# First stage of an attention and convolution backbone: c's rows on another queue, earlier weight roundings, context tiles on ScalarE, ropes on VectorE, and gates ahead of queries

## The chip, the core and the metric

The kernel runs on one core of a Trainium2 chip. The metric is the device time in microseconds of one execution on that core, from its start to its end. Engines are named as in the profile: PE (TensorE, the matmuls), DVE (VectorE), ACT (ScalarE), POOL (GpSimd) and SP (SyncE, which here only issues transfers). DMA transfers are issued by an engine into its own queue; this kernel uses SP's and ACT's.

## The reference

Two layers work on 1024 latent tokens `x` and 256 context tokens `ctx`, both 1024 wide. Layer 0 is attention with 16 query heads in 4 groups that share keys and values (head width 128); layer 1 is a convolution module. What matters here is the way into layer 0:

```python
# per layer: x += gate * Mixer(RMSNorm(x) * (1 + scale) + shift)
# (shift, scale, gate) = Linear_i(SiLU(c))      for latent tokens
# (shift, scale, gate) = Linear_i(SiLU(c_ctx))  for context tokens
proj = h_lat @ w_in
q = apply_rope(split_heads(proj[..., :q_end], N_Q_HEADS), cos, sin)
k = apply_rope(split_heads(proj[..., q_end:k_end], N_KV_HEADS), cos, sin)
v = split_heads(proj[..., k_end:v_end], N_KV_HEADS)
z = proj[..., v_end:]
kv_c = h_ctx @ w_in[:, q_end:v_end]
o = windowed_attention(q, k, v, kc, vc, sink)
y = (o * jax.nn.silu(z)) @ w_out

def apply_rope(x, cos, sin):       # x1, x2: the halves of a head
    return concatenate([x1 * cs - x2 * sn, x2 * cs + x1 * sn])
```

All of it is fp32. `z` is the gate of a head's output.

## The kernel before, in words

**Precision.** PE's fast fp32 format (F32R) keeps fewer bits, so a value is split into a rounded high part and the low part that is left (`whi`/`wlo` for weights, `hh`/`hl` for x, `hch`/`hcl` for the context, `kh`/`kl` and `qh`/`ql` for keys and queries, `ahi`/`alo` for the modulation weights). The high part is a copy on ACT, the low part a subtraction (`split_lo`) on DVE or POOL. A product is three matmuls (`mm3`): high by high, high by low, low by high.

**Memory.** SBUF is handed out in 45 pages of 1024 words and 6 halves of 528 (`Pages`); a tile's name carries `page` or `half` and, in the listings of the order, its running number. PSUM tiles are `pss` (two of two banks), `psg` (two) and `pso` (two).

**Order.** Between `pin("PVAG")` (L334) and `pin("P")` (L607) PE, DVE, ACT and POOL keep the order in which the code is written: this is the first stage. Behind it only PE keeps the written order, and a scheduler places the instructions of the others. Every instruction is recorded at line 90, where a helper issues it, so groups are told apart by their tiles.

**The first stage.** SP loads half of x's rows (`xs0`), the weights of modulation block 0 (`ada_load`, `araw`), weight chunks, and so on in the order in which it is written. ACT's queue loads `c`, `c_ctx`, the identity, the norm weights, `sel` and `sink` (L174 to L179). The rows of `c`, `c_ctx` and the norm weights lie in one tile, `crow`. PE runs five fillers (`idle`: matmuls of zeros `zr` by zeros, 128 x 512, whose result nobody reads), turns `crow` into columns (one transpose), and ACT makes SiLU of it. 28 more fillers follow (L342). Then:

- `ada_mm(pr)` multiplies the columns with four pages of modulation weights, for one of four blocks `pr` of 256 channels. A few of these pages are used as plain fp32 (`ADA_FP`: all of block 0 and two each of blocks 1 and 2), the others are split by `ada_split`. The result is a row of 512 in PSUM, copied to the tile `arow` half by DVE and half by ACT. `ada_cols` turns it into columns `mod` (shift and scale).
- `square` and `normalise` scale rows of x or ctx by 1/rms, `turn` transposes them by PE, and `x_tiles` scales and shifts the result by `mod` on DVE (`hf`), rounds on ACT (`hh`) and subtracts on DVE (`hl`). `c_tile` does the same for a context tile, whose low part is made on POOL (tiles 0 to 5) or DVE (tiles 6 and 7).
- `x_mm(kt, half, acc, which)` adds K tile `kt` (of 8) to the projections k, q and v of the first group, for one half of the tokens (512).
- `WStream` streams weight chunks of 128 columns. `wsA.load()` issues a load on SP, `wsA.split()` rounds the next chunk on ACT and subtracts on DVE (chunks 1 to 3) or POOL; with a list as argument it leaves the subtraction to a later call. The first three chunks are k, q and v of group 0.
- `rope_start` copies a projection out of PSUM by ACT, issues two transfers on ACT's queue that swap the halves of the head (the rotated copy, `rope_half<-rope_half` or `rope_page<-rope_page`, 64 x 512 each), and multiplies by the cosine on DVE. `rope_end` multiplies the rotated copy by the sine on POOL, adds on DVE, rounds on ACT and subtracts on POOL.

The code of the stage ends with the ropes of the first half (k and q, L601), the last x projections, and the split of the fourth weight chunk.

**Behind the stage.** From L1107 on, `enqueue` lists the chunks of the next projections, in the order in which they were added to the list of chunks (L269 to L280), and `fill(n)` runs n matmuls of that list. Nine such matmuls of the fourth chunk run first (`fill(9)`, L1111); behind them come the context's products with k and v of group 0 (`gemm_ctx`, 24 matmuls of 256 columns each), the ends of the first ropes, and the turn of v (`tails`, whose source is `vf`). Then come 16 heads of 8 query blocks each: `scores` two blocks ahead, fillers of 12 projection matmuls in each step of the first four heads, softmax, `pv`. Before, a head's list is q of the next head and then the gate z of this one; two steps before head h + 1 begins, what is left of its q is run (`fill(1000, ...)`). From head 1 on, `low_parts` (L717) also sends the low parts of layer 0's output weights and of the convolution's to DRAM.

## Time and profile before

| | |
|---|---|
| time, 3 runs | median 1775.41 us (1773.73 to 1775.61) |
| the profiled execution | 1776.85 us, of which the span of the profile is 1775.0 |
| mean clock granted to PE | 0.994 |
| PE busy | 1729.6 us, 97% of the span |
| DVE, POOL, ACT busy | 1143.9, 922.2 and 861.6 us |
| PE's share of the first of 40 slices (44.4 us) | 8 tenths |
| HBM traffic | 188.70 MB read, 41.69 MB written, 130 GB/s over the span |

The profile is one execution, taken apart by a hardware profiler; the times of the runs come without it. Its views are a page of totals, and answers of the trace: the waits of an engine (what it waited for, by tile), the timeline of an engine in a window, tables of short windows with the granted clock of PE, and a tile's own instructions. A row of a timeline has the start, the duration, the engine, the operation with the tile written and the tiles read, the number of like instructions in the row, and in brackets how long the engine was idle before it and what ended that. ACTq and SPq are the instructions by which ACT and SP issue transfers.

### The profile page before, as it was taken

What the parts mean: (1) busy time and instruction counts of PE and PEld (TensorE: products, weight loads), DVE (VectorE), ACT (ScalarE), POOL (GpSimd) and SP (SyncE); (2) the same over time, 40 slices, a digit from 0 to 9 for tenths busy, and PEclk for the clock granted to TensorE, in tenths of its full rate; (3) what the DMA queues carried; (4) which work ended last, traced back from release to release, by engine and by line L of the source; (5) the groups of instructions that cost most, each with busy time, mean ns of one, the idle gap of its engine ahead of it and who ended that gap; (6) DMA issues with size and microseconds to landing.
All of it is one profiled execution on the core that took longest, in us unless ns stands there. A gap on an engine that the chain in (4) does not pass through costs nothing.

```text
span 1775.0 us, 23838 instructions
## 1 busy us (share of the span) xinstructions
PE 1729.6 (97%) x8420; PEld 1425.6 (80%) x8420; DVE 1143.9 (64%) x2076; ACT 861.6 (49%) x1409; POOL 922.2 (52%) x836
## 2 busy tenths in 40 slices
PE   8989899999999999999999999999999999999997
PEld 4668788888888888887888888888888888787886
DVE  3755553665556554565314269999999999867833
ACT  5444353545444443444433445564656565466741
POOL 0155555666556646662100247998988888121400
PEclk9989999999999999999999999999999999999999
DMA  9233443354434542435777733011121212377871
GB/s 318 83 94 107 126 136 89 113 166 138 122 107 131 161 145 66 135 105 185 266 260 244 261 95 107 25 48 36 36 84 36 84 36 72 124 244 238 310 281 48
DMA packets 195324, 242.45 MB, mean 137 GB/s; under 512 B 11798, under 2 KB 126790, under 8 KB 195204
## 3 DMA queue, kind: packets, MB, share of 16 engines
q1 hardware_dynamic: 188164, 230.01, 39.7%
q10 hardware_dynamic: 7040, 10.91, 2.5%
q8 instruction: 66, 1.08, 0.3%
q14 instruction: 54, 0.44, 0.1%
HBM read 188.70 MB, written 41.69 MB: 130 GB/s over the span
## 4 chain that ended last, share of the span: by engine, by line
PE 69%; DMA 3%; DVE 2%; issue 1%; ACT 1%; POOL 1%; ACTq 0%; SPq 0%; DVEq 0%; POOLq 0%
PE psg L90 34%; PE pss L90 17%; PE pso L90 17%; DMA low_page<-in_conv_w_out_dram 1%; DMA rope_half<-rope_half 1%; DMA ozf_page<-ozd 1%; DVE mask_page L90 1%; DMA wo_page<-in_conv_w_out_dram 0%; POOL rope_half L90 0%; DVE p_page L90 0%; DVE rope_half L90 0%; DVE ptlo L90 0%; DMA wolC<-low_page 0%; DMA dww_raw<-in_ada_w_dram 0%; POOL p_page L90 0%
## 5 line engine op out<-in xcount | busy, mean ns | idle before, releaser
L90 POOL TENSOR_TENSOR odd_half<-odd_half,prod_half 128x513 f32<-128x513 f32 (+2 forms) x252 | 313.0, 1250 | 24.2 <-ACT prod_half L90 10.9
L90 PE MATMUL psg<-hh_page,whi_page 128*128 128x512 f32 x608 | 241.3, 397 | 3.1 <-ACT whi_page L90 3.1
L90 PE MATMUL psg<-hh_page,wlo_page 128*128 128x512 f32 x608 | 240.5, 396 | 3.5 <-DVE wlo_page L90 3.5
L90 POOL TENSOR_TENSOR wlo_page<-wraw_page,whi_page 128x1024 fp32r<-128x1024 f32 x71 | 175.5, 2473 | 125.8 <-ACT whi_page L90 88.6
L90 PE MATMUL psg<-hl_page,whi_page 128*128 128x512 f32 x608 | 240.4, 395 | 0.0
L90 ACT ACTIVATE prod_half<-ubuf,dww 128x513 f32<-128x513 f32 (+2 forms) x252 | 165.3, 674 | 110.5 <-POOL odd_half L90 108.3
L90 PE MATMUL psg<-h2h_page,whi_page 128*128 128x512 f32 x464 | 184.0, 396 | 0.0
L90 PE MATMUL psg<-h2l_page,whi_page 128*128 128x512 f32 x464 | 182.8, 394 | 0.0
L90 PE MATMUL psg<-h2h_page,wlo_page 128*128 128x512 f32 x464 | 182.5, 393 | 0.0
L90 POOL TENSOR_SCALAR p_page<-p_page,sc 128x640 f32<-128x640 f32 (+1 forms) x128 | 100.9, 789 | 145.9 <-DVE sc L90 145.2
L90 DVE SCALAR_TENSOR_TENSOR pss<-ubuf,dww,pss 128x512 f32<-128x512 f32 (+3 forms) x270 | 172.6, 672 | 0.1
L90 DVE SCALAR_TENSOR_TENSOR pss<-ubuf,wsum,pss 128x512 f32<-128x512 f32 (+3 forms) x270 | 171.9, 672 | 0.2
L90 ACT ACTIVATE p_page<-p_page,sc 128x641 f32<-128x641 f32 (+1 forms) x128 | 102.7, 802 | 92.9 <-DVE sc L90 73.7
L90 ACT ACTIVATE pthi<-pss 128x640 fp32r<-128x640 f32 (+1 forms) x144 | 88.7, 616 | 114.9 <-PE pss L90 106.0
L90 DVE TENSOR_TENSOR ptlo<-pss,pthi 128x640 fp32r<-128x640 f32 (+1 forms) x144 | 103.2, 716 | 63.5 <-ACT pthi L90 62.5
L90 PEld LDWEIGHTS psg<-hh_page,wlo_page 128*128 128x128 f32 x608 | 114.9, 189 | 27.7 <-DVE wlo_page L90 4.3
L90 PEld LDWEIGHTS psg<-hh_page,whi_page 128*128 128x128 f32 x608 | 114.8, 189 | 26.2 <-ACT whi_page L90 3.5
L90 PEld LDWEIGHTS psg<-hl_page,whi_page 128*128 128x128 f32 x608 | 115.1, 189 | 21.5
L90 ACT ACTIVATE whi_page<-wraw_page 128x1024 fp32r<-128x1024 f32 x88 | 92.5, 1052 | 63.9 <-PE psg L90 29.1
L90 PE MATMUL pso<-h2h_page,whi_page 128*128 128x512 f32 x304 | 119.7, 394 | 0.0
L90 PE MATMUL pso<-h2l_page,whi_page 128*128 128x512 f32 x304 | 119.6, 393 | 0.0
L90 PE MATMUL pso<-h2h_page,wlo_page 128*128 128x512 f32 x304 | 119.5, 393 | 0.0
(256 smaller groups left out, 4079.0 us busy)
## 6 DMA issues: line engine op xcount, KB each, us to landing
wraw_page<-in_conv_w_in_dram SPq DMA_DIRECT2D x48, 512.0 KB, 4.0
wraw_page<-in_attn_w_in_dram SPq DMA_DIRECT2D x40, 512.0 KB, 4.6
wol_page<-wolA SPq DMA_DIRECT2D x32, 512.0 KB, 5.5
wo_page<-in_attn_w_out_dram SPq DMA_DIRECT2D x32, 512.0 KB, 7.4
wo_page<-in_conv_w_out_dram SPq DMA_DIRECT2D x32, 512.0 KB, 5.7
wol_page<-wolC SPq DMA_DIRECT2D x32, 512.0 KB, 6.8
rope_half<-rope_half ACTq DMA_DIRECT2D x76, 128.0 KB, 2.5
araw_page<-in_ada_w_dram SPq DMA_DIRECT2D x32, 256.0 KB, 5.8
```

What stands on the lines that cost most here:

```text
L90: r = f(*a, **k)
```

## The change

All of it concerns the order of work and the engine that does it; the arithmetic stays.

1. The loads of `c` and `c_ctx` move from ACT's queue to SP's, ahead of x's rows.
2. `idle(28)` becomes `idle(29)`, and `idle(4)` behind `ada_split(1)` goes.
3. The first two weight splits move ahead of `ada_mm(0)`, and the copy of a modulation row is made by DVE alone, 512 wide.
4. The two split pages of modulation block 2 are made together (earlier for the second), the first two of block 3 behind the x tiles of K tile 4 instead of ahead of `ada_cols(2)`.
5. Context tiles are scaled and shifted on ACT (Identity with scale and bias) instead of DVE.
6. The fourth weight chunk is split right behind the last `x_tiles` instead of ahead of `x_mm(7, 1)`.
7. The first four ropes have their product with the sine and their last subtraction on DVE instead of POOL.
8. In the first group (heads 0 to 3) a head's gate z is projected ahead of the next head's q: the chunk list and the places that enqueue agree on it.

```diff
-    A.dma_start(out=crow[0:8], in_=c.rearrange("o (r p) -> (o r) p", p=P))
-    A.dma_start(out=crow[8:16], in_=c_ctx.rearrange("(r p) -> r p", p=P))
+    SY.dma_start(out=crow[0:8], in_=c.rearrange("o (r p) -> (o r) p", p=P))
+    SY.dma_start(out=crow[8:16], in_=c_ctx.rearrange("(r p) -> r p", p=P))
...
-            zq.insert(1 if h % 4 == 3 else 0, (("q", h + 1), wcol((h + 1) * P)))
+            zq.insert(1 if h < 4 or h % 4 == 3 else 0, (("q", h + 1), wcol((h + 1) * P)))
...
-    idle(28)
+    idle(29)
...
-            V.tensor_copy(R[pr][0:4, 0:256], o[0:4, 0:256])
-            act(R[pr][0:4, 256:512], o[0:4, 256:512], AF.Copy)
+            V.tensor_copy(R[pr][0:4, 0:512], o[0:4])
...
-        modulated(turn(cx, kt, lambda: ps_o(bank))[:, 0:CT], [(h, l, lambda f: f[:, 0:CT])],
-                  m[:, 2 + i, 1:2], m[:, i, 1:2], CT, V if kt >= 6 else G)
+        tp = turn(cx, kt, lambda: ps_o(bank))
+        f = pg.alloc(F32, [1024], "hf")
+        act(f[:, 0:CT], tp[:, 0:CT], AF.Identity, scale=m[:, 2 + i, 1:2], bias=m[:, i, 1:2])
+        act(h, f[:, 0:CT], AF.Copy)
+        split_lo(V if kt >= 6 else G, l, f[:, 0:CT], h)
+        pg.free(f)
...
-    def rope_end(started, sl, dh, dl, eng):
+    def rope_end(started, sl, dh, dl, eng, rest=G):
         pool, pgs, w, r = started
-        tt(G, w, w, sin[:, sl], ALU.mult)
+        tt(rest, w, w, sin[:, sl], ALU.mult)
         tt(eng, r, r, w, ALU.add)
         act(dh, r, AF.Copy)
-        split_lo(G, dl, r, dh)
+        split_lo(rest, dl, r, dh)
...
+    low = []
+    wsA.split()
+    wsA.split(low)
     ada_mm(0)
     tps = [turn(xs0, kt, lambda: acc1[kt]) for kt in range(2)]
-    wsA.split()
     ada_cols(0)
-    low = []
-    wsA.split(low)
     x_tiles((tps[0], 0, 0, V), (tps[1], 1, 0, V))
     low.pop()()
     ada_split(1)
-    idle(4)
...
-    ada_split(2, (2,))
+    ada_split(2)
...
-    ada_split(2, (3,))
...
-    ada_split(3, range(2))
...
     x_tiles((tp, 4, 0, V), (tq, 4, 1, V))
+    ada_split(3, range(2))
...
     x_tiles((tp, 6, 1, V), (tq, 7, 1, V))
+    wsA.split()
     pg.free(*xs1)
...
-    wsA.split()
     x_mm(7, 1, acc1, range(3))
     pin("P")
...
+    enqueue(("z", 0))
     enqueue(("q", 1))
-    enqueue(("z", 0))
     fill(9)
...
-    rope_end(rk0, lo, *(t[:, lo] for t in d0[0]), V)
+    rope_end(rk0, lo, *(t[:, lo] for t in d0[0]), V, V)
...
-                for key in ((("z", n), ("q", n + 1)) if n % 4 == 3 else (("q", n + 1), ("z", n))):
+                for key in ((("z", n), ("q", n + 1)) if n < 4 or n % 4 == 3 else (("q", n + 1), ("z", n))):
```

Three places show how instructions move. The first is the beginning of the program on ACT, then on SP; `crow` holds the rows of c, c_ctx and the norm weights. ACT before:

```order
L90 DMA crow_half_75<-in_c_dram 8x128
L90 DMA crow_half_75<-in_c_ctx_dram 8x128
L90 DMA ident<-in_k_ident_dram 128x128
L90 DMA crow_half_75<-in_norm_g_dram 16x128
L90 DMA sel<-in_k_sel_dram 128x2
L90 DMA sink<-in_attn_sink_dram 128x16
```

SP now:

```order
L90 DMA crow_half_75<-in_c_dram 8x128
L90 DMA crow_half_75<-in_c_ctx_dram 8x128
L90 DMA x_page_84<-in_x_dram 128x1024
L90 DMA x_page_85<-in_x_dram 128x1024
L90 DMA x_page_86<-in_x_dram 128x1024
L90 DMA x_page_87<-in_x_dram 128x1024
```

The two rows of c stand at the head of SP's queue, ahead of x's four; on ACT's, the identity is now first and the norm weights second.

The second place is ACT at the end of the stage: `hch` are the context's high parts, `vf` a copy of v, `rope` the copies for the ropes, and `whi<-wraw` the rounding of the fourth weight chunk. Before:

```order
L90 ACTIVATE hch_page_756<-hf_page_761 128x256
L90 ACTIVATE hch_page_756<-hf_page_768 128x256
L90 ACTIVATE rope_half_772<-pss_157 128x512
L90 DMA rope_half_773<-rope_half_772 64x512 x2
L90 ACTIVATE rope_page_779<-pss_157 128x512
L90 DMA rope_page_780<-rope_page_779 64x512 x2
L90 ACTIVATE hch_page_756<-hf_page_798 128x256
L90 ACTIVATE vf_half_888<-psg_161 128x512
L90 ACTIVATE hch_page_756<-hf_page_805 128x256
L90 ACTIVATE whi_page_809<-wraw_page_714 128x1024
```

Now:

```order
L90 ACTIVATE hh_page_679<-hf_page_718 128x512
L90 ACTIVATE hh_page_684<-hf_page_721 128x512
L90 ACTIVATE whi_page_726<-wraw_page_707 128x1024
L90 ACTIVATE hf_page_733<-pso_730,mod_206 128x256
L90 ACTIVATE hch_page_642<-hf_page_733 128x256
L90 ACTIVATE hf_page_740<-pso_737,mod_206 128x256
L90 ACTIVATE vf_half_836<-psg_160 128x512
L90 ACTIVATE hch_page_642<-hf_page_740 128x256
```

The rounding of the chunk stands right behind the last two roundings of x (`hh`), ahead of the last four context tiles and of the rope copies; each context tile now has two rows on ACT, `hf` and `hch`.

The third place is DVE at the same time: `rope` with `cos` and `sin` are the products, `rope<-rope,rope` the sums, `hcl` the low parts of context tiles 6 and 7, and `wlo` that of the fourth chunk. Before:

```order
L90 TENSOR_TENSOR rope_half_774<-pss_157,cos_page_580 128x512
L90 TENSOR_TENSOR rope_page_781<-pss_157,cos_page_580 128x512
L90 TENSOR_SCALAR hf_page_798<-pso_795,mod_207 128x256
L90 TENSOR_TENSOR hcl_page_757<-hf_page_798,hch_page_756 128x256
L90 TENSOR_SCALAR hf_page_805<-pso_802,mod_207 128x256
L90 TENSOR_TENSOR rope_half_774<-rope_half_774,rope_half_773 128x512
L90 TENSOR_TENSOR hcl_page_757<-hf_page_805,hch_page_756 128x256
L90 TENSOR_TENSOR rope_page_781<-rope_page_781,rope_page_780 128x512
L90 TENSOR_TENSOR wlo_page_810<-wraw_page_714,whi_page_809 128x1024
```

Now:

```order
L90 TENSOR_TENSOR wlo_page_727<-wraw_page_707,whi_page_726 128x1024
L90 TENSOR_TENSOR rope_half_771<-pss_157,cos_page_574 128x512
L90 TENSOR_TENSOR rope_page_778<-pss_157,cos_page_574 128x512
L90 TENSOR_TENSOR rope_half_770<-rope_half_770,sin_page_575 128x512
L90 TENSOR_TENSOR rope_half_771<-rope_half_771,rope_half_770 128x512
L90 TENSOR_TENSOR rope_page_777<-rope_page_777,sin_page_575 128x512
L90 TENSOR_TENSOR hcl_page_754<-hf_page_795,hch_page_753 128x256
L90 TENSOR_TENSOR rope_page_888<-pss_158,cos_page_574 128x512
L90 TENSOR_TENSOR rope_page_778<-rope_page_778,rope_page_777 128x512
L90 TENSOR_TENSOR kl_page_830<-rope_half_771,kh_page_829 128x512
L90 TENSOR_TENSOR hcl_page_754<-hf_page_802,hch_page_753 128x256
```

The chunk's low part stands ahead of all ropes; the low parts of context tiles 6 and 7 stand behind products with the sine, and the second behind a rope's last subtraction (`kl`), which were POOL's before.

More of the change, by code (lines that the diff above doesn't have):

```diff
@@ L1113, in backbone_kernel @@
     run(gemm_ctx(wsA.hl[0], o))
-    rope_end(rk0, lo, *(t[:, lo] for t in d0[0]), V)
+    rope_end(rk0, lo, *(t[:, lo] for t in d0[0]), V, V)
     tails.append(finish("v", 0, 1, acc1[2], d0[2]))
-    rope_end(rq0, lo, *(t[:, lo] for t in d0[1]), V)
+    rope_end(rq0, lo, *(t[:, lo] for t in d0[1]), V, V)
     rq1 = rope_start(acc1[1], hi, pg)
@@ L1122, in backbone_kernel @@
     tails.append(finish("v", 0, 2, o, d0[2]))
-    rope_end(rq1, hi, *(t[:, hi] for t in d0[1]), V)
-    rope_end(rk1, hi, *(t[:, hi] for t in d0[0]), V)
+    rope_end(rq1, hi, *(t[:, hi] for t in d0[1]), V, V)
+    rope_end(rk1, hi, *(t[:, hi] for t in d0[0]), V, V)
     for i in range(3):
```

## The prediction

> **What bounds the kernel now.** I read the page first, then PE's waits up to 130 us, then the timelines of that stretch by engine, and last PE's waits later on.
>
> ```profile
> PE 1729.6 (97%) x8420; PEld 1425.6 (80%) x8420; DVE 1143.9 (64%) x2076; ACT 861.6 (49%) x1409; POOL 922.2 (52%) x836
> ```
>
> PE is busy for 97% of the span, so only time in which PE waits, runs slowly, or runs fillers can be won. The list of PE's waits up to 130 us (us in total, times, longest) shows where the first stage loses it:
>
> ```profile
> PE psg L90 <- DVE wlo_page L90: 3.5, 1, 3.5
> PE psg L90 <- DMA crow_half<-in_norm_g_dram: 3.3, 1, 3.3
> PE psg L90 <- ACT whi_page L90: 3.1, 1, 3.1
> PE pso L90 <- ACT vf_half L90: 2.2, 1, 2.2
> ...
> PE pso L90 <- DVE mod L90: 1.4, 1, 1.4
> ```
>
> Two places matter. The first is the start, in PE's timeline (start, us, engine, operation):
>
> ```profile
> 1.92 2.50 PE L90 MATMUL psg<-zr_half 128*128 128x512 f32 x5 [1.92 <-DVE zr_half L90]
> 7.75 0.28 PE L90 MATMUL psg<-ident,crow_half 32*128 32x32 f32 x1 [3.33 <-DMA crow_half<-in_norm_g_dram]
> 7.97 8.27 PE L90 MATMUL psg<-zr_half 128*128 128x512 f32 x28
> 16.17 7.03 PE L90 MATMUL pso<-araw_page,cf 128*4 128x512 f32 x16
> 23.13 1.10 PE L90 MATMUL pss<-ident,x_page 128*128 128x128 f32 x8
> ```
>
> PE turns c's rows at 7.75, after their last transfer, then runs 28 fillers, and only behind those the first modulation matmuls (16.17 to 23.13). Everything later in the stage hangs on 23.13. The second place is the end of the stage, again PE's timeline:
>
> ```profile
> 90.36 0.39 PE L90 MATMUL psg<-hl_page,whi_page 128*128 128x512 f32 x1
> 90.59 0.40 PE L90 MATMUL psg<-hh_page,wlo_page 128*128 128x512 f32 x1
> ...
> 105.06 0.28 PE L90 MATMUL pso<-hch_page,wlo_page 128*128 128x256 f32 x1
> 105.18 0.28 PE L90 MATMUL pso<-hch_page,whi_page 128*128 128x256 f32 x1
> ...
> 112.12 0.66 PE L90 MATMUL pso<-ident,vf_half 128*128 128x128 f32 x4 [2.18 <-ACT vf_half L90]
> ```
>
> Between 90.98 (the end of the x projections) and 112.12 PE has 15 matmuls of 512 columns and 48 of 256. Starts lie 0.23 and 0.12 apart when nothing is awaited, so this is 15 x 0.23 + 48 x 0.12 = 9.2 us of work in 21.1 us: 11.9 us are lost. 8.8 of them are the waits for whi, wlo and vf above. The rest is a slow clock behind those waits, by the table of windows (next to last: granted clock):
>
> ```profile
> 100.00:102.00 2.00, 2.00 (x7) 1.52 (x6) 0.80 (x2) 0.60 (x1) 0.00 (x0) 0.50 0.55 119
> ```
>
> The timeline of all engines shows why the fourth weight chunk came so late:
>
> ```profile
> 92.95 1.04 ACT L90 ACTIVATE whi_page<-wraw_page 128x1024 fp32r<-128x1024 f32 x1
> 93.30 0.69 DVE L90 TENSOR_TENSOR rope_half<-rope_half,rope_half 128x512 f32<-128x512 f32 x1 [0.70 <-POOL rope_half L90]
> ...
> 94.59 1.27 POOL L90 TENSOR_TENSOR rope_page<-rope_page,sin_page 128x512 f32<-128x512 f32 x1 [1.32 <-DMA rope_page<-rope_page]
> ...
> 95.81 1.26 POOL L90 TENSOR_TENSOR kl_page<-rope_half,kh_page 128x512 fp32r<-128x512 f32 x1
> 95.89 1.73 DVE L90 TENSOR_TENSOR rope_page<-rope_page,rope_page 128x512 f32<-128x512 f32 x1 [1.56 <-POOL rope_page L90]
> 97.54 1.21 DVE L90 TENSOR_TENSOR wlo_page<-wraw_page,whi_page 128x1024 fp32r<-128x1024 f32 x1
> ```
>
> The chunk's rounding (whi) stands on ACT behind the copies and transfers of the first ropes, and its low half (wlo) on DVE behind a rope's sum, which waits for POOL's product with the sine.
>
> **The change part by part.** Times below are on before's clock.
>
> *c's rows from SP.* ACT's own start and the landing of a rotated copy (64 x 512 floats; view of the rope tile, 85 to 116 us):
>
> ```profile
> 1.37 0.28 ACTq L90 DMA_DIRECT2D crow_half<-in_c_ctx_dram  x1
> 1.68 0.36 ACTq L90 DMA_DIRECT2D ident<-in_k_ident_dram  x1
> 2.08 0.45 ACTq L90 DMA_DIRECT2D crow_half<-in_norm_g_dram  x1
> ```
>
> ```profile
> DMA to landing us min/median/max: 2.9/3.5/4.1
> ```
>
> The norm weights, which end the wait, were issued at 2.08, behind three of the four large row transfers, and were there at 7.7: 5.6 us. Now they are ACT's second transfer, so at about 1.37, and the rows of x start behind c's two on SP. At 2.9 us they land at 4.3, and PE turns c when its first five fillers end, at 4.42. At 5.6 us they land at 7.0. I take the first, since the large transfers no longer run ahead of them. The 29 fillers then begin at 4.65. As slow at their start as the 28 were (8.20), with one more of 0.23, they end at 13.1; all at 0.23 they end at 11.3. The modulation matmuls take 6.96 more: 18.3 to 20.1. Their data bound this: SP issued the transfers of these weights up to 10.72 (the last six in its timeline, 0.54 each), and they land after (view of their tile)
>
> ```profile
> 7.92 3.26 SPq L90 DMA_DIRECT2D araw_page<-in_ada_w_dram  x6
> ...
> DMA to landing us min/median/max: 4.3/5.8/7.1
> ```
>
> that is by 17.8, or 18.7 behind two small issues (0.9 us). The last quarter of the matmuls (1.74) would then end at 20.4 at the latest. I take 19.4: a gain of 3.7 us against 23.13, with 2.7 to 4.8 as bounds, and 0.5 if the norm weights still need 5.6 us (7.04 + 0.22 + 8.43 + 6.96 = 22.65).
>
> The Trainium skill has a rule on the fillers ("TensorE: Matmul & The Clock Gate", Part 1): PE's clock is halved after an idle window of about 3.4 us and full again after as long a busy one. By it the 3.3 us gap at 4.42 cost a second slow start; without the gap the fillers could end at about 11.6, and the sum would be 1 us better than mine. The row of 28 fillers (8.27 us instead of 28 x 0.23 = 6.4) agrees.
>
> *Weight roundings ahead, one copy of the modulation row on DVE, four fillers fewer.* In the first three rows these stand in ACT's idle time before 23.13. The path from there (turns, columns, scale, rounding) is the same. I cost them at 0, between 0.2 lost (one 512-wide copy for two halves) and 0.3 won.
>
> *Middle of the stage.* The waits for mod (1.4) and two smaller ones go, since two roundings of the last modulation block now stand behind the x tiles of block 4. But DVE does as much as before, and the same roundings must be done for PE's last modulation block:
>
> ```profile
> 69.58 2.36 DVE L90 TENSOR_TENSOR alo_page<-araw_page,ahi_page 128x1024 fp32r<-128x1024 f32 x2 [0.26 <-ACT ahi_page L90]
> ```
>
> ```profile
> 74.25 1.52 POOL L90 TENSOR_SCALAR x_page<-x_page,r 128x1024 f32<-128x1024 f32 x1 [46.76 <-DVE r L90]
> ```
>
> Replayed in the new order with DVE's own durations, these two end at 72.0, as before (71.9), and the context rows are scaled at 75.9 (before 75.8), which PE then awaits. So I take 0; the bound is 2.2 won, if DVE were not the limit.
>
> *Context tiles on ACT, fourth chunk early, ropes on DVE.* The chunk's whi now follows the last x rounding on ACT (84 to 85) and its low half ends near 86, well before 91: the waits of 3.1 and 3.5 and the slow clock go, and with them the whole 11.9, unless something else is late. It is: context tiles 6 and 7 have their low halves on DVE behind the ropes. PE would reach their matmuls at 95.4 and 96.6. ACT issues q's rotated copy up to 92.9 (second transfer at 92.25; lands 2.9 later, 95.15); DVE's product (0.69) and then tile 6's half end at 96.2: 0.8 us of wait. Tile 7's half stands behind three more operations of 0.69 and ends at 98.5: 1.9 us. PE is through both context products at 101.7, and turns v at 103.05 instead of 112.12 (bank freed at 102.2): 9.1 us won. Bounds: 11.9 with no wait, 6.0 if the copies land after 4.1 us (1.2 for each of two) and the clock falls behind these waits (3.4 us at half speed, the rest of the bound).
>
> In the rows above DVE's sum took 1.73 us beside POOL's subtraction and 0.69 alone. The Trainium skill ("SBUF — State Buffer", Who interferes with whom) says that a DVE operation with two SBUF inputs blocks against a POOL operation that reads SBUF; the two rows agree. By this rule the eight rope operations stay at 0.69, as I count them, since the change leaves POOL no rope work there; at 1.73 each the sum would be some 4 us worse.
>
> *Gate leads.* In the first four heads the matmuls are as many, but head h+1's q now comes behind gate h. Its first half ends near step 3 of 8 and is wanted at step 6.
>
> ```profile
> 146.57 0.36 PE L90 MATMUL pss<-kh_page,qh_page 128*128 128x256 f32 x1
> ```
>
> ```profile
> 214.44 0.57 ACT L90 ACTIVATE rope_half<-psg 128x512 f32<-128x512 f32 x1
> ```
>
> ```profile
> 226.46 1.31 POOL L90 TENSOR_TENSOR ql_page<-rope_half,qh_page 128x512 fp32r<-128x512 f32 x1
> ```
>
> By before's steps the half would end at 133.7 and be wanted at 146.6: 12.9 us, against up to 13.3 for a rope (214.44 to 227.77). So 0 to 0.4 for each of three heads. The stall here that the reshuffled rows may remove is
>
> ```profile
> 212.71 1.23 PE L90 MATMUL pss<-ident,p_page 128*128 128x128 f32 x5 [3.35 <-DVE sc L90]
> ```
>
> which I leave at 0 both ways, with 4.5 won (3.4 and its slow clock) as a bound.
>
> **Sum.** 3.7 + 0 + 9.1 + 0 = 12.8 us. The profiled execution took 1776.85 us (span 1775.0 and 1.85 around it); the median of the runs is 1775.41. 1776.85 - 12.8 = 1764.05, and from the median **1762.6**.
>
> **The rivals.** (1) The norm weights still land late: 0.5 + 9.1 = 9.6, 1765.8. For it: the queues share engines that were full at that time. Against: the big transfers start later. (2) Context halves wait longer on the rope copies: 3.7 + 6.0 = 9.7 at the bound, and 1768 if a wait of the middle comes back as well (1.4 and 1.0 in ACT's longer queue). (3) The stall at 212 goes too: 12.8 + 4.5, 1758.1. (4) The other side: gate leads starves the scores. Place: the first scores of heads 1, 2 and 3, for want of q. Price: whatever a rope takes over 12.9 us, three times, with 1.7 us of slow clock behind each. From 15.5 us a rope (2.6 + 1.7, three times) it eats the gain; at 19 us it costs 3 x (6.1 + 1.7) = 23.4 and gives 1786.0. For it: POOL works off these ropes between the softmax's rows. Against: the slowest rope seen took 13.3.
>
> **How the numbers follow.** A measurement of this kernel can tell about 0.2%, 3.6 us, from no change. Chances: forecast 0.58, (1) 0.15, (2) 0.12, (3) 0.09, (4) 0.06. Cases that win over 3.6 us hold 0.94; of these I move 0.01 to "same" for the stretch between (2) and (4), and of (4) 0.01. So faster 0.93, same 0.02, slower 0.05. The forecast's own range is 1759.5 to 1765, from its bounds. Taking in (1), most of (2) and (3) gives 1757.5 to 1768.5, which leaves out (4) and the edges.
>
> **What would show it.** Right: PE turns c before 5 us; the x rows are turned near 19.4 instead of 23.13, and the first x matmul comes as much earlier; the last modulation matmuls still wait about 2 us on alo; no wait on whi or wlo of the fourth chunk, the clock full from 90 us on, and small waits on hcl instead; v turned near 99 on the new clock. Wrong: c turned after 7 us; waits over 4 us for hcl or rope tiles; scores of heads 1 to 3 waiting on ql.

## The result and the profile after

| | before | after |
|---|---|---|
| time | 1775.51 us median of 4 runs (1773.73 to 1778.43) | 1756.86 us median of 4 runs (1756.38 to 1762.61) |
| ratio of the times | | 0.9901, 95% interval 0.9876 to 0.9925 |
| the profiled execution, its span | 1776.85, 1775.0 us | 1756.40, 1754.2 us |
| mean clock granted to PE | 0.994 | 0.995 |

The change wins 18.65 us between the medians; the ratio makes 17.6 of it, with 13.3 to 22.0 as its interval. 12.8 were forecast, just below that interval. By the ratio the time stands at 1757.8 on the scale of the prediction, at the lower edge of its range (1757.5 to 1768.5); the median itself lies 0.6 below it. The changed kernel was measured a second time, beside other kernels: 1757.76 us, ratio 0.9891 (0.9879 to 0.9904).

The waits of PE up to 130 us in the changed kernel (columns: us in total, times, longest):

```profile
PE pso L90 <- DVE vl_page L90: 2.1, 1, 2.1
...
PE pss L90 <- ACT hh_page L90: 1.9, 1, 1.9
PE pso L90 <- DVE hcl_page L90: 1.5, 1, 1.5
PE pso L90 <- ACT hh_page L90: 0.7, 1, 0.7
PE pso L90 <- POOL x_page L90: 0.7, 1, 0.7
PE pso L90 <- DVE alo_page L90: 0.6, 1, 0.6
```

The waits for the norm weights, for whi and wlo of the fourth chunk, for mod and for the copy of v are gone. New are one for `vl` (the low part of v, 2.1), a longer one for the first rounded x (`hh`, 1.9, before 0.8), one for `hcl`, and two of 0.7 in the middle of the stage (a second `hh`, and rows scaled by POOL). PE's timeline at the start:

```profile
1.92 2.50 PE L90 MATMUL psg<-zr_half 128*128 128x512 f32 x5 [1.92 <-DVE zr_half L90]
4.34 0.31 PE L90 MATMUL psg<-ident,crow_half 32*128 32x32 f32 x1
4.59 8.30 PE L90 MATMUL psg<-zr_half 128*128 128x512 f32 x29
12.82 7.03 PE L90 MATMUL pso<-araw_page,cf 128*4 128x512 f32 x16
19.78 1.09 PE L90 MATMUL pss<-ident,x_page 128*128 128x128 f32 x8
20.80 1.05 PE L90 MATMUL pso<-sel,arow_half 5*128 5x2 f32 x8
23.74 0.50 PE L90 MATMUL pss<-hh_page,whi_page 128*128 128x512 f32 x1 [1.89 <-ACT hh_page L90]
```

c is turned at 4.34 without a wait, x at 19.78. Behind the columns (20.80) PE now waits 1.89 us where before it ran the four fillers and then waited 0.77. The table of short windows of the changed kernel (the last three columns are the granted clock, the DMA share and GB/s) shows what follows, and the same again near 77 us:

```profile
24.00:26.00 2.00, 1.78 (x5) 1.26 (x5) 1.97 (x3) 1.27 (x2) 0.00 (x0) 0.69 1.11 341
26.00:28.00 2.00, 2.00 (x4) 0.25 (x4) 1.71 (x3) 1.26 (x2) 0.00 (x0) 0.50 1.19 326
...
76.00:78.00 2.00, 2.00 (x11) 1.80 (x9) 0.57 (x1) 0.65 (x2) 0.96 (x2) 0.50 0.00 0
78.00:80.00 2.00, 2.00 (x8) 1.58 (x7) 1.65 (x3) 1.26 (x2) 0.00 (x0) 0.66 0.00 0
90.00:94.00 4.00, 4.00 (x22) 3.25 (x21) 2.08 (x3) 2.99 (x7) 0.18 (x1) 1.00 0.64 145
94.00:98.00 4.00, 2.50 (x21) 2.30 (x21) 3.73 (x8) 2.08 (x5) 0.49 (x1) 1.00 0.27 59
```

In the kernel before the clock was 1.00 from 24 to 28 and from 76 to 80, and it was low from 92 to 100, where the changed kernel has 1.00 up to 98:

```profile
92.00:96.00 4.00, 1.22 (x2) 0.50 (x2) 1.74 (x5) 2.09 (x4) 2.68 (x3) 0.67 0.37 109
96.00:100.00 4.00, 1.19 (x3) 1.00 (x4) 3.34 (x3) 1.23 (x2) 2.62 (x2) 0.50 0.00 0
```

PE's timeline of the changed kernel at the end of the stage, with what it waits for in brackets:

```profile
90.85 0.39 PE L90 MATMUL psg<-hh_page,wlo_page 128*128 128x512 f32 x1
...
97.49 0.39 PE L90 MATMUL pso<-hcl_page,whi_page 128*128 128x256 f32 x1 [1.50 <-DVE hcl_page L90]
...
102.05 0.60 PE L90 MATMUL pso<-ident,vf_half 128*128 128x128 f32 x4
...
103.18 0.28 PE L90 MATMUL pss<-kh_page,qh_page 128*128 128x256 f32 x1
...
107.30 0.44 PE L90 MATMUL pso<-ident,vf_half 128*128 128x128 f32 x2 [2.12 <-DVE vl_page L90]
```

Reading the same points off PE's timelines of both kernels gives where the 20.8 us between the two spans arise (this pair of executions lies 2.1 us further apart than the medians):

| PE starts | before | after | won so far |
|---|---|---|---|
| turn of x (first) | 23.13 | 19.78 | 3.35 |
| turn of x (second) | 35.63 | 33.57 | 2.06 |
| last x projection | 90.59 | 90.85 | -0.26 |
| turn of v | 112.12 | 102.05 | 10.07 |
| first scores of head 0 | 113.30 | 103.18 | 10.12 |
| first scores of head 4 | 308.49 | 294.57 | 13.92 |
| first scores of head 12 | 700.16 | 682.56 | 17.60 |
| end of the span | 1775.0 | 1754.2 | 20.8 |

So there are three gains (start, end of the stage, heads) and one loss, of 3.6 us, between the turn of x and the last x projection.

### The profile page after: what moved, and what is told of

It reads as the page before. It is cut to its first block, busy times and chain, and to the rows that moved or that the text cites. A ratio compares the mean times of both kernels' runs of the same rounds, so it can differ in the third digit from the quotient of the medians.

```text
span 1754.2 us, 23817 instructions
## 1 busy us (share of the span) xinstructions
PE 1726.0 (98%) x8417; PEld 1424.5 (81%) x8417; DVE 1148.2 (65%) x2076; ACT 865.9 (49%) x1413; POOL 911.6 (52%) x828
## 4 chain that ended last, share of the span: by engine, by line
PE 72%; DVE 2%; DMA 2%; issue 1%; ACT 1%; POOL 0%; SPq 0%; DVEq 0%; ACTq 0%
PE psg L90 37%; PE pss L90 18%; PE pso L90 17%; DMA low_page<-in_conv_w_out_dram 1%; DVE mask_page L90 1%; DMA ozf_page<-ozd 0%; DVE p_page L90 0%; DVE ptlo L90 0%; DMA wolA<-low_page 0%; DMA wolC<-low_page 0%; DMA dww_raw<-in_ada_w_dram 0%; POOL low_page L90 0%; ACT pthi L90 0%; POOL p_page L90 0%; DVE pss L90 0%
```

## The experiments

The kernels were measured in three groups, each on another chip and beside the kernel before (its medians: 1776.2, 1777.55 and 1777.79 us), and they are compared by their ratio to it. 0.001 is 1.8 us. The changed kernel, in the third group, stands at 0.9891 (0.9879 to 0.9904). With intervals of this width a difference between two kernels is uncertain by some 4 us.

| kernel | median us | ratio to before, 95% interval |
|---|---|---|
| changed, c's rows on ACT's queue | 1761.74 | 0.9917, 0.9899 to 0.9934 |
| changed, fourth chunk split late | 1766.87 | 0.9942, 0.9926 to 0.9958 |
| changed, q ahead of z | 1770.60 | 0.9957, 0.9942 to 0.9972 |
| changed, four fillers back | 1757.99 | 0.9887, 0.9867 to 0.9907 |
| changed, ropes on POOL | 1757.60 | 0.9891, 0.9872 to 0.9911 |
| changed, context tiles on DVE | 1756.08 | 0.9882, 0.9864 to 0.9899 |
| before, z ahead of q alone | 1767.93 | 0.9955, 0.9937 to 0.9973 |
| before, fourth chunk early alone | 1772.32 | 0.9970, 0.9957 to 0.9983 |
| changed, three additions | 1756.43 | 0.9880, 0.9862 to 0.9898 |
| changed, q ahead of z, low rows a step later | 1768.79 | 0.9953, 0.9942 to 0.9965 |
| changed, fillers back, low rows a step later | 1762.29 | 0.9916, 0.9905 to 0.9928 |

**c's rows back on ACT.**

```diff
-    SY.dma_start(out=crow[0:8], in_=c.rearrange("o (r p) -> (o r) p", p=P))
-    SY.dma_start(out=crow[8:16], in_=c_ctx.rearrange("(r p) -> r p", p=P))
+    A.dma_start(out=crow[0:8], in_=c.rearrange("o (r p) -> (o r) p", p=P))
+    A.dma_start(out=crow[8:16], in_=c_ctx.rearrange("(r p) -> r p", p=P))
```

> The changed kernel with c's two rows back on ACT's queue; all else as changed. My theory (the norm weights land late because they were issued behind c's rows and beside the large row transfers): PE turns c between 7 and 8 us again instead of at 4.34, x is turned near 23.1 instead of 19.78, everything behind it moves with it, and the time is 3.0 to 3.6 us over the changed kernel's. Rival (in the changed kernel the weight loads are then what is awaited, so the lateness is absorbed by the fillers or by the waits of the middle): c is turned late, but by the context products (93.16) less than 1.5 us of it is left.

PE's timeline of this kernel:

```profile
7.75 0.28 PE L90 MATMUL psg<-ident,crow_half 32*128 32x32 f32 x1 [3.33 <-DMA crow_half<-in_norm_g_dram]
7.96 8.81 PE L90 MATMUL psg<-zr_half 128*128 128x512 f32 x29
...
23.66 1.09 PE L90 MATMUL pss<-ident,x_page 128*128 128x128 f32 x8
```

The wait is back to the hundredth. x is turned 3.88 us later than in the changed kernel, and head 0's first scores come at 107.16, 3.98 later: nothing is absorbed on the way to them. The ratio says 4.6 us, more than the 3.0 to 3.6 expected, but it is uncertain by nearly as much. The first theory holds for the mechanism.

**The fourth chunk's split back.**

```diff
     x_tiles((tp, 6, 1, V), (tq, 7, 1, V))
-    wsA.split()
...
+    wsA.split()
     x_mm(7, 1, acc1, range(3))
```

> The changed kernel with the split of the fourth weight chunk back ahead of the last x projections; all else as changed, ropes and context tiles too. My theory (the split's place in ACT's order was the cause): the waits on whi and wlo of the fourth chunk come back, over 4 us together, with a slow clock behind them; 6 to 9 us over the changed kernel's time. Rival (the ropes' products on POOL held up DVE, and with them gone the split is in time wherever it stands): waits under 2 us together, less than 3 us over.

PE's timeline, then ACT's:

```profile
97.22 0.80 PE L90 MATMUL psg<-hh_page,whi_page 128*128 128x512 f32 x1 [6.86 <-ACT whi_page L90]
...
99.52 0.79 PE L90 MATMUL psg<-hh_page,wlo_page 128*128 128x512 f32 x1 [1.07 <-DVE wlo_page L90]
```

```profile
95.28 0.63 ACT L90 ACTIVATE kh_page<-rope_half 128x512 fp32r<-128x512 f32 x1 [2.19 <-DVE rope_half L90]
...
96.13 1.04 ACT L90 ACTIVATE whi_page<-wraw_page 128x1024 fp32r<-128x1024 f32 x1
```

The wait for whi is longer than in the kernel before, since the chunk now also stands behind a rope's rounding (`kh`) that awaits DVE. Head 0's first scores come at 110.83, 7.65 later; the time is 9 us over by the ratio. Counted from the last x projection (89.98 here, 90.85 in the changed kernel), the first scores come 8.5 us later, since this execution was 0.9 us ahead up to there. The split's place is what mattered, and not POOL's ropes.

**That move alone, on the kernel before.** The edit is the reverse of the one above.

> The kernel before with the fourth weight chunk's split moved up behind the last x tiles, and nothing else of the change. Theory one (the split's place is the whole of the stage end's gain, wherever the ropes and context tiles stand): the waits of 3.06 and 3.54 us on whi and wlo go, the clock stays full from 92 us on, and the first scores come 6 to 9 us earlier than at 113.30. What the time makes of it depends on the heads behind, whose stall near 212 the kernel keeps: by theory one it is 6 to 9 us under the kernel before. Theory two (an earlier first stage runs into the same stalls of heads 0 to 2 and gives some back, as it did with q ahead of z, where all else together won only 5.6): under 5 us.

Head 0's first scores come at 105.64, 7.66 earlier than before, as theory one has it. But the time falls by 5.3 us only (interval 3.0 to 7.6), and PE's waits up to 130 us begin with

```profile
PE pso L90 <- DVE vl_page L90: 3.4, 1, 3.4
```

which before has not. The first scores of head 4 come at 302.92, 5.57 earlier than before: some of the gain went into the first heads. The time lies between the two theories (6 to 9, and under 5), nearer to the second, and its interval does not tell them apart. The profiled execution was the fastest of nine (1766.61 us, median 1772.32), so the trace does not show where the usual one lost the rest. It also had a slow clock in the middle of the stage (0.50 from 64 to 66 us), which the edit does not touch, and a wait of 0.8 for `hf`, which DVE now makes behind the moved subtraction; it reached the last x projection only at 93.68 (before 90.59). From there to the first scores it took 11.96 us, before 22.71: at this place the move is worth 10.75.

**Ropes back on POOL; context tiles back on DVE.** Two kernels, an edit each.

```diff
-    rope_end(rk0, lo, *(t[:, lo] for t in d0[0]), V, V)
+    rope_end(rk0, lo, *(t[:, lo] for t in d0[0]), V)
```

(and the other three), and

```diff
-        act(f[:, 0:CT], tp[:, 0:CT], AF.Identity, scale=m[:, 2 + i, 1:2], bias=m[:, i, 1:2])
-        act(h, f[:, 0:CT], AF.Copy)
-        split_lo(V if kt >= 6 else G, l, f[:, 0:CT], h)
...
+        modulated(turn(cx, kt, lambda: ps_o(bank))[:, 0:CT], [(h, l, lambda f: f[:, 0:CT])],
+                  m[:, 2 + i, 1:2], m[:, i, 1:2], CT, V if kt >= 6 else G)
```

> The changed kernel with the sine products and the last subtractions of the first four ropes back on POOL; all else as changed. Theory one (the ropes had to leave POOL: the chain through POOL is longer, and DVE's sums are slow beside it): the low parts of context tiles 6 and 7 come no earlier on DVE, and the first scores wait over 2 us for a kl or ql made on POOL; 2 to 5 us over the changed kernel's time. Theory two (with the fourth chunk out of the way POOL does them as well): the wait on hcl falls from 1.50 to under 0.6, no wait takes its place, and the time is within 1.5 us of the changed kernel's, or below it.

> The changed kernel with the context tiles scaled and shifted on DVE again; all else as changed. Theory one (DVE is the late engine at the stage's end, so what leaves it counts): tiles 6 and 7 get their hf behind the rope products on DVE, the wait on the context's high or low parts grows from 1.5 to over 2.5 us, and the time is 1 to 3 us over the changed kernel's. Theory two (the eight operations hide on either engine): the waits there stay within 0.5 us, and so does the time within 1.2.

With the ropes on POOL, PE's list of waits has

```profile
PE pso L90 <- DVE hcl_page L90: 2.8, 2, 2.5
```

(1.5 in the changed kernel), but no wait for vl. Head 0's first scores come 2.06 us later (105.24) and head 1's 0.5 earlier (138.55 against 139.08). From the last x projection (90.03) to the first scores it took 15.2 us, the changed kernel 12.3: at the stage's end the ropes on DVE do gain 2.9 us, but by head 1 nothing is left of them. With the context tiles on DVE the wait for `hcl` is gone altogether, one of 0.8 for `hf` takes its place earlier, and head 0's first scores come 1.56 us earlier (101.62). By the ratio the two times lie 0 and 1.6 us off the changed kernel's. No expectation of the waits was met in full, but on the time theory two is the nearer one twice: these two parts of the change are worth nothing that can be measured in the time.

**q ahead of z again, and z ahead of q alone.** The first edit puts back the chunk list, the two `enqueue` lines and the condition of the loop in the changed kernel; the second makes just these changes in the kernel before.

```diff
-            zq.insert(1 if h < 4 or h % 4 == 3 else 0, (("q", h + 1), wcol((h + 1) * P)))
+            zq.insert(1 if h % 4 == 3 else 0, (("q", h + 1), wcol((h + 1) * P)))
```

> The changed kernel with q ahead of z again in the first group; all else as changed. The stall of 3.35 us near 212 (behind a low-part transfer) is gone in the changed kernel, and 6 us with it. Theory one (gate leads removed it, since POOL and ACT then have no rope to do beside the low parts at that place): the stall comes back near 200, over 2.5 us, and heads 2 to 3 take 5 to 6 us more; the wait of 2.1 us on vl stays. Theory two (the stall goes by any shift in time of the transfers): it stays away, and the time is within 2.5 us of the changed kernel's.

> The kernel before with gate z ahead of the next q in the first group, and nothing else of the change. Theory one (the stall of 3.35 us near 212, and the slow clock behind it, come from the order of q and z alone, by way of the page that the next low row is given): the stall is gone, heads 2 to 3 take 5 to 6 us less, the waits of the first stage are all there, and the time is 6 to 12 us under the kernel before. Theory two (the order of q and z helps only on top of the earlier first stage): less than 3 us under it, with a stall of over 2 us in heads 1 to 3.

PE's waits between the first scores of head 0 and those of head 4, first in the kernel before, next in the changed one with q ahead, then in the kernel before with z ahead:

```profile
PE pss L90 <- DVE sc L90: 3.6, 2, 3.4
PE pss L90 <- DVE ptlo L90: 1.1, 1, 1.1
```

```profile
PE pss L90 <- DVE sc L90: 5.9, 4, 3.8
PE pss L90 <- DVE ptlo L90: 1.4, 1, 1.4
...
```

```profile
PE pso L90 <- DVE ptlo L90: 0.8, 1, 0.8
```

The stretch takes 195.2 us in the kernel before and 189.7 with z ahead, 191.4 in the changed kernel and 200.7 with q ahead. In the time, z ahead alone wins 8 us by the ratio, and taking it back costs 11.7. Both times it is the order of q and z that decides, with the first stage late or early. Theory one, and for the undone order more than it priced: heads 2 and 3 take 7.9 us more with q ahead, not 5 to 6. Its wait for vl did not stay (0.4 in place of 2.1). The times of this kernel spread widely (1764.02 to 1772.49), and the profiled execution was the slowest of nine.

How a stall arises, the ACT queue shows. The changed kernel with q ahead, ACT's timeline at the stall:

```profile
201.12 0.63 ACT L90 ACTIVATE qh_page<-rope_half 128x512 fp32r<-128x512 f32 x1 [2.38 <-POOL rope_half L90]
206.45 0.63 ACT L90 ACTIVATE lhi_half<-low_page 128x512 fp32r<-128x512 f32 x1 [4.70 <-DMA low_page<-in_attn_w_out_dram]
206.99 0.36 ACT L90 ACTIVATE pthi<-pss 128x256 fp32r<-128x256 f32 x1
```

ACT stands first at the rounding of the next q, which POOL's sum holds up, then at a low row that has not landed; the softmax's rounding (`pthi`) stands behind. DVE waits 5.8 us for that rounding (up to 207.38) with the next block's softmax behind it, and PE's next work, the turn of that block, waits for DVE: the 3.8 us in the list above. The load itself came late: SP issued it at 202.24, after 3.9 us of waiting for the store of the low row before it, whose page it was given (SP's waits; kernel before, then this one):

```profile
SPq L90 <- DMA wolA<-low_page: 4.4, 2, 3.3
```

```profile
SPq L90 <- DMA wolA<-low_page: 4.9, 2, 3.9
```

In the changed kernel and in the kernel before with z ahead SP has no such wait in that stretch, and ACT's wait for low rows falls (in the changed kernel measured again it is 6.6). ACT's rows for this, in the kernel before, with q ahead, in the changed kernel, and in the kernel before with z ahead:

```profile
ACT lhi_half L90 <- DMA low_page<-in_attn_w_out_dram: 12.1, 6, 4.2
```

```profile
ACT lhi_half L90 <- DMA low_page<-in_attn_w_out_dram: 12.5, 5, 4.7
```

```profile
ACT lhi_half L90 <- DMA low_page<-in_attn_w_out_dram: 5.4, 4, 3.6
```

```profile
ACT lhi_half L90 <- DMA low_page<-in_attn_w_out_dram: 7.0, 5, 3.7
```

Not every such wait costs something. The changed kernel has one of 3.62 us as well, and PE does not wait near it, since the softmax's rounding of that step (`pthi`, 188.95) stands ahead of it:

```profile
188.95 0.60 ACT L90 ACTIVATE pthi<-pss 128x512 fp32r<-128x512 f32 x1 [0.23 <-PE pss L90]
193.18 0.63 ACT L90 ACTIVATE lhi_half<-low_page 128x512 fp32r<-128x512 f32 x1 [3.62 <-DMA low_page<-in_attn_w_out_dram]
```

**Low rows a step later.** With q ahead as above, the rounding of the first five low rows is put one step behind:

```diff
-        for src, dst in items:
+        for n, (src, dst) in enumerate(items):
...
             yield "open"
+            if n < 5:
+                yield "open"
             for b in range(2):
```

> The changed kernel with q ahead of z in the first group (1770.6 us as such) and one more step between the load of a low row and its rounding on ACT, for the first five rows. Theory one (the stall of heads 2 and 3 is ACT standing at the rounding of a low row that has not landed, with the softmax's rounding behind it in its queue): the stall of 3.8 us near 209 and that of 1.4 near 189 go, heads 2 to 3 lose under 2 us in place of 8.6, and the time is 5 to 10 us below 1770.6, so within 3 to 8 us of the changed kernel's. Theory two (q ahead of z is slow by its ropes on POOL, and the low row only stands nearby): the time stays within 3 us of 1770.6.

ACT's waits in the same stretch, first with q ahead (its wait for low rows, 12.5, stands above), then with low rows later as well:

```profile
ACT qh_page L90 <- POOL rope_half L90: 17.9, 6, 5.2
```

```profile
ACT qh_page L90 <- POOL rope_half L90: 22.4, 6, 6.9
...
ACT lhi_half L90 <- DMA low_page<-in_attn_w_out_dram: 5.2, 4, 2.1
```

The low row's wait is more than halved, and the stall of 3.8 near 209 is gone. But ACT now stands 6.9 us at the rounding of q, PE waits 2.3 us near 206 instead, and the stretch is only 1.1 us shorter (199.5). The ratio is the same as without the edit. Theory one fails as a whole: the low row was one of two things at which ACT stood ahead of the softmax, and the other, the rope of the next q, remains. With z ahead of q the wait for low rows falls, but the one at the rounding of q does not; in the changed kernel it is

```profile
ACT qh_page L90 <- POOL rope_half L90: 17.7, 6, 4.8
```

So if the ropes have a part in the 8 to 11.7 us, it is by where these waits fall and not by their sum. That is not shown here: the order of q and z is the cause of the gain, and by what share the low rows and by what the ropes carry it stays open.

**The fillers back, and the fillers with low rows later.**

```diff
     ada_split(1)
+    idle(4)
     x_mm(0, 0, acc0, (0,))
```

> The changed kernel with the four fillers back behind the first x tiles' turn; all else as changed. In the changed kernel PE waits 1.89 us there (before 0.77), and the granted clock is 0.59 from 24 to 28 us (before 1.00). Theory one (the fillers kept the clock up, and cost nothing as they ran inside a wait): the wait falls under 1.0, the clock stays at 1.00, PE's first x matmuls start 0.23 apart, and the second turn of x comes 1 to 2 us earlier than 34.33; the time is 1 to 2 us below the changed kernel's. Theory two (the clock falls for want of work before that, in the columns and turns, whatever stands in the wait): the clock is low from 24 to 28 again and the time is within 0.5 us.

> The changed kernel with the four fillers back and one more step between the load and the rounding of the first five low rows. Theory one (what is won early was given back in heads 2 to 4 by waits on low rows): the 1.7 us won by the fillers at the first scores are still there at head 4, and the time is 1.5 to 4 us below the control's. Theory two (what is given back depends on the rotated copies and the regroupings further on): the time is within 1.5 us of the control's.

Windows of the first kernel:

```profile
24.00:26.00 2.00, 1.79 (x6) 0.87 (x7) 1.97 (x3) 1.01 (x2) 0.00 (x0) 1.00 1.11 341
26.00:28.00 2.00, 2.00 (x6) 0.43 (x5) 1.48 (x3) 1.26 (x2) 0.00 (x0) 1.00 1.18 322
```

Here the clock stays up, the second turn of x comes at 31.78 (changed kernel 33.57; the 34.33 of the expectation is not in its trace), and head 0's first scores 1.70 us earlier. At head 4 nothing is left of it (294.92 against 294.57), and the time is that of the changed kernel. With the low rows later too, the clock fell in spite of the fillers (0.65 and 0.50 in the two windows), head 3 met waits of 0.7 and 1.8 us for `ptlo` and a rope, and the kernel is 4.4 us slower than the changed one: neither theory has that. On the clock theory one of the first expectation is not shown: of six profiled kernels with the four fillers it stayed full in three (before, before with the chunk early, this one) and fell in three; of the eight without, it fell in all. Where it fell, the fillers won nothing: from the first to the second turn of x it took 13.8 us in this kernel and in the one with three additions below, as in the changed kernel without them (13.79), and 12.26 in the first kernel, where it stayed full. On what is won early, theory two of the second expectation is the nearer one, and its bound was too narrow.

**Three additions.** The changed kernel with the fillers, and

```diff
-        split_lo(V if kt >= 6 else G, l, f[:, 0:CT], h)
+        split_lo(G, l, f[:, 0:CT], h)
...
-    fill(3)
-    tails[2]()
-    fill(3)
+    fill(6)
     scores(0, 1)
-    fill(4)
+    fill(3)
+    tails[2]()
+    fill(1)
```

> The changed kernel with three additions: the four fillers back, the low parts of context tiles 6 and 7 on POOL (idle there, as the ropes left it), and the turn of the context's v moved behind the second scores. Theory one (PE's time is lost where PE waits, and what is won at head 0's first scores stays won): no wait over 0.5 us on hcl or vl, the clock full from 24 to 32 us, head 0's first scores 3 to 5 us earlier than at 103.18, and 3 to 5 us under the changed kernel's time. Theory two (the heads behind give it back, as they seemed to with the fillers alone): the first scores are earlier, but head 4 begins less than 2 us earlier than at 294.57, and the time is within 2 us.

The wait for `hcl` is gone and that for `vl` is 0.7. The clock fell again (0.60 and 0.55), so head 0's first scores come 1.85 us earlier and not 3 to 5. They are 1.93 earlier at head 4 (292.64) and 0.8 later at head 12 (683.37). The time equals the changed kernel's within the uncertainty; theory two. No kernel of these beats it by more than the measurement is uncertain.

**The changed kernel again.**

> The changed kernel once more, unaltered, beside the kernel before on this chip: the yardstick for the three kernels beside it. If the gain is what the first measurement said, it is 16 to 21 us under the kernel before here as well, and its first scores come near 103.2 and head 4 near 294.6; if those were chance, they lie elsewhere.

1757.76 us, 20.0 below the kernel before (1777.79; 19.4 by the ratio); head 0's first scores at 102.85, head 4's at 294.72. The gain holds.

## Why the prediction was right in direction and short in size

The time lies in the range, but not by the forecast's own sum: it is past the narrower range of the forecast itself (1759.5 to 1765) and nearest to rival (3) (1758.1, chance 0.09). Part of that is luck: a gain priced at 0 was larger than rival (3) had it, and 3.6 us of losses that the sum did not have took some of it back. Term by term:

1. *c's rows: right.* 3.7 won were forecast, 3.35 came, 3.88 when undone; in the ten profiled kernels with c's rows on SP x is turned at 19.23 to 19.78, where 19.4 was said. The norm weights were in time (the first of the two values). In this execution the modulation matmuls were not held up by their data, and the fillers were as slow as assumed: 29 in 8.30 us. On the gap ahead of the fillers one pair misleads, since 28 took 8.27 before. Against 0.23 us each, the fillers took 0.6 to 1.6 us more in the ten kernels without the gap (mean 1.1), and 1.5 to 2.5 more in the four with it (mean 2.0). The estimate of 1 us that the prediction made from the Trainium skill ("TensorE: Matmul & The Clock Gate", Part 1) for the gap of 3.3 us agrees with these means. Not all of that is a gain: in four of the executions with faster fillers the modulation matmuls waited 0.2 to 0.8 us for their data.
2. *Four fillers fewer, at 0 between 0.2 lost and 0.3 won: wrong by 1.3.* Between the first and the second turn of x 1.3 us were lost, by a clock that fell to 0.50 behind the wait. The prediction looked only at the wait in which the fillers ran, and had no term for the clock. That the missing fillers let it fall is not shown: it also fell in three of six kernels that have them.
3. *Middle, at 0: wrong by 2.3.* PE waits for the last modulation block as said, though less (0.7 ahead of it and 0.6 for alo, "about 2 us" forecast), and the mod wait went. But a slow clock between 76 and 80 us, which the sum did not have, took more than the waits gave. It stands behind three short waits (66 to 74 us) and comes and goes between executions: with the same waits it was slow in nine of the eleven profiled kernels that have this part of the change, and full in two, such as the one with ropes on POOL:

```profile
76.00:78.00 2.00, 2.00 (x15) 1.82 (x15) 0.82 (x4) 1.17 (x3) 1.20 (x2) 1.00 0.00 0
```

   From the second turn of x to the last x projection these two took 55.7 us, the changed kernel 57.3 and the kernel before 55.0. So some 1.6 us are the slow clock's, and 0.7 us are lost without it. To which edit these belong no run here shows: the order of the modulation splits was not undone.
4. *Stage end, 9.1 won: right, and 10.3 from the last x projection to the turn of v.* The mechanism is shown by two runs: the chunk's place alone costs 8.5 us when undone and wins 10.75 on the kernel before, from the last x projection to the first scores (7.65 and 7.66 at head 0, where clocks of the middle, unlike from run to run, enter too). The wait for `hcl` was one of 1.5 and not 0.8 and 1.9, and the clock did not fall behind it. The wait of 2.1 for `vl`, behind the first scores, was not foreseen. The lower bound was added up wrongly: 1.2 twice and 3.4 us at half speed take 4.1 from 9.1 and leave 5.0, not 6.0. Of the other two edits that the term counted, the ropes give 2.9 us here that the heads take back, and the context tiles none. The rope operations took 0.68 to 0.69 on DVE, as counted, but for one beside POOL's subtraction for a weight chunk (106.05 to 108.41):

```profile
107.16 1.79 DVE L90 TENSOR_TENSOR kl_page<-rope_half,kh_page 128x512 fp32r<-128x512 f32 x1
```

   This agrees with the Trainium skill ("SBUF — State Buffer", Who interferes with whom): a DVE instruction with two SBUF inputs contends with a POOL instruction that reads SBUF. The operation just ahead of it (`vl`, 106.56), one of whose inputs lies in PSUM, took 0.69 beside the same subtraction.
5. *Gate leads, at 0 both ways: the step that failed.* The prediction saw the stall at 212 and gave its loss to a rival, at 4.5 us and a chance of 0.09. The order of q and z is worth 8 to 11.7 us. Its argument followed q's deadline (rival 4: scores starved for q), and no score waited on ql. What it missed is the other direction: what stands ahead of the softmax in ACT's queue when q is projected early, above all a low row that is given a page still being stored. With 8 to 11.7 in place of this 0 the forecast's sum would be 20.8 to 24.5, and with the 3.6 us that points 2 and 3 take off 17.2 to 20.9, around what was found. But the terms are not independent. Undone one at a time, c's rows, the chunk's place and the order of q and z cost 4.6, 9.1 and 11.7 us, 25.4 together, more than the whole change wins. And all of the change without the gate's move wins only 7.6 us by the ratio, although its first scores come 8.3 us earlier than before's (104.96 against 113.30): PE's waits in the first four heads are then 7.7 us, against 4.7 before.
6. *Behind head 4, not in the sum.* In this pair another 6.9 us are won after head 4, of which 2.1 are the pair's own distance from the medians. Some of it is a wait for a rope near 680 (0.94 before, none after) that comes and goes between kernels; no run isolates it, and where the rest of it arises is not shown.

## What to carry to other kernels

A stall is priced by what stands behind it in the in-order queue: a rounding that waits for a transfer costs nothing until the softmax's step is queued behind it. When two jobs can be swapped without any deadline in danger, look at what the early one puts ahead of other work in the queues of the other engines, not only at when its result is wanted. And a gain at the front of a kernel is one at the end only if the stages between have the slack to keep it: check the start of each later stage, as the first scores of each head here, before adding terms.

## What was not expected of the hardware

- The granted clock fell to 0.50 behind a wait of only 1.89 us that followed 1 us of matmuls of two columns (20.80 to 28), and fell or stayed full in otherwise like executions: with the same four fillers and the same wait of 0.76 us it was 1.00 in one kernel and 0.60 in another from 24 to 26 us. The same holds near 77 us, behind three waits of 0.6 to 0.7 us. What decides is not settled here. A clock like this moves single executions by 1 to 2 us, so what an edit does to a stage is better read from a mark right ahead of that stage than from the start of the program.
- The rows of the first fillers are slow (five in 2.50 us, where later ones start 0.23 apart), while the granted clock is given as 1.00 there: the column does not show the slow start.
